# Batched 64x64 products: GpSimd issues a tile's load between the halves of its memset, and eight result buffers in place of six

## The chip, the core and the metric

The kernel runs on one core of a Trainium2 chip. The metric is device time in microseconds (us). Lengths inside one execution are read from its profile, whose span (first to last instruction) is shorter than the time by about 1.8 us. In the profile's lines DVE is VectorE, ACT ScalarE, POOL GpSimd and SP SyncE; the DMA queue q0 is GpSimd's, q1 SP's and q10 ACT's. A line of a timeline has start, us, engine, source line, operation, tiles, sizes and count, and in brackets the idle time before it and what ended it.

## The reference

```python
def setup_inputs():
    return {
        "a": np.random.randn(1024, 64, 64).astype(np.float32),
        "b": np.random.randn(1024, 64, 64).astype(np.float32),
    }

def reference(a, b):
    return np.matmul(a, b).astype(np.float32)
```

Each input and the result is 16.78 MB. Some 50.3 MB have to cross HBM.

## The kernel before

The 1024 products go through in sixteen tiles t of 64. Two tiles share one a tile s of 128 matrices, a(0) to a(7). GpSimd loads a(1) to a(7), four pieces each, and converts to bf16 on the way; a(0) is loaded as fp32 by the SP and ACT queues, which also load the b tiles. VectorE regroups an a tile, PE transposes it, ScalarE copies the transposed tile out, and VectorE spreads it into a block-diagonal tile, the stationary operand of the products. ScalarE evacuates the first half of each result tile and VectorE the second. GpSimd issues the stores, held back by one tile.

```python
    A_AHEAD = 3      # buffers of a tiles
    B_AHEAD = 4      # buffers of b tiles
    HOLD = 2         # the store of tile t is issued after tile t+1 is multiplied
    ...
    o_pool = ctx.enter_context(tc.tile_pool(name="o_pool", bufs=6))
    ...
    def load_a(s):
        a_sb = a_pool.tile([128, 4, 16, 64], bf16, name="a_sb")
        for h in range(4):
            nc.gpsimd.dma_start(
                out=a_sb[:, h, :, :].rearrange("p v k -> p (v k)"), in_=a_v[s, h]
            )
    ...
        load_first_a()                                # a(0), SP and ACT queues
        ...
        for t in range(B_AHEAD):
            load_b(t)
        nc.vector.memset(bd_tiles[0][:], 0.0)
        make_identity(nc, identity)                   # GpSimd
        nc.gpsimd.memset(bd_tiles[1][:], 0.0)         # GpSimd, 4096 elements a row
        for s in range(1, A_AHEAD):
            load_a(s)                                 # a(1), a(2)
        ...
        for t in range(n_t):
            ...
            if half == 0:
                if s + 2 < n_s:
                    regroup(s + 2)                    # VectorE, ahead of multiply(t)
                if s + 1 + A_AHEAD < n_s:
                    load_a(s + 1 + A_AHEAD)
            multiply(t)
            ...
            if t >= HOLD - 1:
                store(t - HOLD + 1)
```

## Time and profile before

| | |
|---|---|
| time, median of 4 runs of the first comparison | 135.51 us (135.26 to 135.67) |
| span of the traced execution | 134.0 us |
| VectorE busy | 105.5 us, 79% |
| HBM traffic | 33.55 MB read, 16.78 MB written, 375 GB/s over the span |
| memset on GpSimd | 3.51 us, first a issue at 4.71 us |
| first packet of GpSimd's DMA queue | 8.6 us |

### The profile page before, as it was taken

To read this page: it belongs to the slowest core of one execution; us is meant where nothing else is said; L and a number is where in the kernel's file an instruction comes from. 1 tells how busy PE (TensorE), PEld (TensorE's weight loads), DVE (VectorE), ACT (ScalarE), POOL (GpSimd) and SP (SyncE) were. 2 spreads that over 40 slices of the span, in tenths; PEclk is the share of its full clock that TensorE was granted. 3 is DMA by queue.
4 is the path that set the end of the run, shared out by engine and by line. 5 is a ranking of instruction groups with operands and counts; after the bars stand their busy time and mean duration, and the time that the engine had idled before them with its cause. 6 is when DMAs were issued, how large, how long until landed. Compare 5 with 4: busy or idle time off the path is not lost.

```text
span 134.0 us, 2820 instructions
## 1 busy us (share of the span) xinstructions
PE 66.2 (49%) x1152; PEld 61.9 (46%) x1152; DVE 105.5 (79%) x145; ACT 86.4 (64%) x125; POOL 43.7 (33%) x55
## 2 busy tenths in 40 slices
PE   0008206903970495849734863696309564466300
PEld 0008106904960485749624752685209463456300
DVE  5720539169899989998999999999299999999940
ACT  3244343991899287959998796679708999363500
POOL 8981215332313240214322244324004031141460
PEclk9999975797799768686998699559955999555555
DMA  3999999999999999999999999999999999999793
GB/s 67 386 360 305 306 284 273 267 301 305 302 280 289 281 396 332 310 289 350 402 359 279 269 367 399 351 270 275 390 397 395 393 397 398 402 406 362 262 313 112
DMA packets 17484, 43.17 MB, mean 322 GB/s; under 512 B 1088, under 2 KB 1088, under 8 KB 17472
## 3 DMA queue, kind: packets, MB, share of 16 engines
q0 software_dynamic: 8448, 24.12, 61.7%
q1 hardware_dynamic: 6624, 13.63, 28.7%
q10 hardware_dynamic: 2400, 5.24, 10.3%
q8 instruction: 9, 0.15, 0.4%
q14 instruction: 3, 0.02, 0.0%
HBM read 33.55 MB, written 16.78 MB: 375 GB/s over the span
## 4 chain that ended last, share of the span: by engine, by line
DMA 62%; DVE 14%; issue 11%; POOL 9%; POOLq 1%; DVEq 0%
DMA a_sb<-in_a_dram 45%; DMA out_dram<-o_sb 17%; DVE o_sb L165 8%; DVE at_bd L121 6%; POOL out_dram L154 3%; POOL a_sb L67 3%; POOL at_bd L205 3%; POOLq L262 1%; POOL identity masks.py:199 0%; DVE a_bf L99 0%; POOL identity masks.py:197 0%; POOLq L154 0%; DVEq L99 0%; POOLq masks.py:199 0%; DVEq L121 0%
## 5 line engine op out<-in xcount | busy, mean ns | idle before, releaser
L177 PEld LDWEIGHTS <-at_bd 128*128 128x128 bf16 x1024 | 43.8, 114 | 45.3 <-DVE o_sb L165 30.4
L177 PE MATMUL o_ps<-b_bf,at_bd 128*128 128x64 bf16 x960 | 43.1, 215 | 40.2 <-DVE o_sb L165 28.5
L121 DVE COPY at_bd<-at_sb 32x1024 f32<-32x1024 f32 x64 | 46.6, 728 | 7.3 <-ACT at_sb L111 5.3
L165 ACT COPY o_sb<-o_ps 64x512 f32<-64x512 f32 x60 | 34.8, 580 | 17.4 <-PE o_ps L177 10.7
L165 DVE COPY o_sb<-o_ps 64x512 f32<-64x512 f32 x60 | 41.3, 689 | 2.2 <-PE o_ps L177 1.3
L154 POOL DMA_DIRECT2D out_dram<-o_sb x20 | 20.9, 1044 | 46.6 <-DVE o_sb L165 22.8
L108 PE MATMUL at_ps<-identity,a_bf 128*128 128x128 f32 x128 | 22.8, 339 | 17.6 <-ACT a_bf L97 10.6
L67 POOL DMA_DIRECT2D a_sb<-in_a_dram x28 | 18.7, 681 | 38.9 <-DMA a_sb<-in_a_dram 28.1
L132 ACT CAST b_bf<-b_sb 128x2048 bf16<-128x2048 f32 x15 | 28.6, 1908 | 3.5 <-DMA b_sb<-in_b_dram 3.5
L108 PEld LDWEIGHTS at_ps<-identity,a_bf 128*128 128x128 f32 x128 | 19.1, 181 | 17.9 <-issue 10.6
L111 ACT COPY at_sb<-at_ps 128x512 f32<-128x512 f32 x32 | 17.8, 588 | 8.3 <-PE at_ps L108 8.1
L99 DVE COPY a_bf<-a_sb 128x4096 bf16<-128x4096 bf16 x7 | 8.6, 1227 | 9.0 <-DMA a_sb<-in_a_dram 8.8
L97 ACT CAST a_bf<-o_sb 128x1024 bf16<-128x1024 f32 x2 | 2.1, 1044 | 4.6 <-DMA o_sb<-in_a_dram 4.6
L165 ACT COPY o_sb<-at_ps 64x256 f32<-64x256 f32 x8 | 2.9, 367 | 3.1 <-PE at_ps L177 3.0
L177 PE MATMUL at_ps<-b_bf,at_bd 128*128 128x64 bf16 x64 | 3.6, 242 | 1.3 <-DVE at_bd L121 1.3
L203 DVE MEMSET at_bd<- 128x4096 f32 x1 | 3.5, 3472 | 0.8 <-issue 0.8
L97 DVE CAST a_bf<-o_sb 128x1024 bf16<-128x1024 f32 x2 | 1.5, 764 | 3.0 <-DMA o_sb<-in_a_dram 3.0
L205 POOL MEMSET at_bd<- 128x4096 f32 x1 | 3.5, 3509 | 0.0
L165 DVE COPY o_sb<-at_ps 64x256 f32<-64x256 f32 x8 | 3.4, 422 | 0.1
L200 ACT ACT_TABLE_LOAD x1 | 1.3, 1283 | 2.3 <-issue 2.3
L139 ACT CAST b_bf<-b_sb 128x512 bf16<-128x512 f32 x2 | 1.1, 614 | 0.4 <-DMA b_sb<-in_b_dram 0.4
L137 DVE CAST b_bf<-b_sb 128x512 bf16<-128x512 f32 x2 | 0.8, 426 | 0.0
(9 smaller groups left out, 1.5 us busy)
## 6 DMA issues: line engine op xcount, KB each, us to landing
out_dram<-o_sb POOLq DMA_DIRECT2D x14, 1024.0 KB, 22.5
a_sb<-in_a_dram POOLq DMA_DIRECT2D x28, 256.0 KB, 19.9
o_sb<-in_a_dram ACTq DMA_DIRECT2D x2, 512.0 KB, 6.9
o_sb<-in_a_dram SPq DMA_DIRECT2D x2, 512.0 KB, 5.9
out_dram<-o_sb POOLq DMA_DIRECT2D x2, 512.0 KB, 6.2
out_dram<-o_sb POOLq DMA_DIRECT2D x4, 256.0 KB, 3.9
b_sb<-in_b_dram SPq DMA_DIRECT2D x12, 0.5 KB, 20.2
b_sb<-in_b_dram ACTq DMA_DIRECT2D x4, 0.5 KB, 16.2
```

Source lines behind the costliest of these rows:

```text
L67: nc.gpsimd.dma_start(out=a_sb[:, h, :, :].rearrange("p v k -> p (v k)"), in_=a_v[s, h])
L97: copy(a_bf[:, :, h, :], a_sb[h].rearrange("p (v k) -> p v k", v=16))
L99: nc.vector.tensor_copy(a_bf[:], a_sb[:].rearrange("p h v k -> p v h k"))
L108: nc.tensor.transpose(at_ps[:, vo, :], a_cols[:, 4 * vo + 2 * j + wl, :], identity[:])
L111: nc.scalar.copy(at_tiles[s][:, j, :, wl, :, :], at_ps[:].rearrange("p vo (g mp) -> p g mp vo", mp=4),)
L121: nc.vector.tensor_copy(bd[rows, :, :, :, h, :].rearrange("p j g wl mo -> p j (g wl) mo"), at_tiles[t // 2][rows, :, half, :, :, :].rearrange(
L132: nc.scalar.copy(b_bf[:], b_sb[:])
L154: nc.gpsimd.dma_start(out=o_v[t, :, lo : lo + n, :], in_=o_sb[:, lo : lo + n].rearrange("p gh j wl n -> p (gh j wl n)"),)
L165: copy(dst, src)
L177: nc.tensor.matmul(o_ps[:, gl, g % 2, j, :], at_bd[:, j, g, :, u], b_bf[:, g, 64 * u : 64 * u + 64], start=(u == 0), stop=(u == 1),)
L203: nc.vector.memset(bd_tiles[0][:], 0.0)
L205: nc.gpsimd.memset(bd_tiles[1][:], 0.0)
```

## The change

GpSimd's 3.5 us memset stood in front of all its a loads. The change cuts it in two and issues a(1) between the halves; a(2) still follows the second half. Two more result buffers are to let evacuation run further ahead of the stores.

```diff
-    o_pool = ctx.enter_context(tc.tile_pool(name="o_pool", bufs=6))
+    o_pool = ctx.enter_context(tc.tile_pool(name="o_pool", bufs=8))
...
-        nc.gpsimd.memset(bd_tiles[1][:], 0.0)
-        for s in range(1, A_AHEAD):
+        nc.gpsimd.memset(bd_tiles[1][:, 0], 0.0)
+        load_a(1)
+        nc.gpsimd.memset(bd_tiles[1][:, 1], 0.0)
+        for s in range(2, A_AHEAD):
             load_a(s)
```

## The prediction

> **What bounds the kernel now.** I read the page's slices first, then the chain of waits, then VectorE's timeline where the chain names it, then the queues stretch by stretch.
>
> ```profile
> DVE  5720539169899989998999999999299999999940
> DMA  3999999999999999999999999999999999999793
> ```
>
> The DMA row is full from the second slice (a slice is 134.0/40 = 3.35 us) to the third from the end. VectorE is ragged for eight slices (27 us), then full to the end with one hole, the 2 in slice 29. So there are two limits that nearly agree: the transfers over the whole span, and VectorE from about 28 us on. The chain says what starts VectorE and what makes the hole:
>
> ```profile
> 1.31 3.46 POOL at_bd L205
> 4.76 3.83 POOL a_sb L67 x7
> 8.59 19.32 DMA a_sb<-in_a_dram
> ...
> 76.67 19.88 DMA a_sb<-in_a_dram
> ```
>
> The columns are start, us, what. The chain begins with GpSimd's 3.46 us memset, goes through its eight DMA issues, and then waits 19.32 us for the last piece of the second tile that they load, a(2). VectorE's own lines show the same two landings, 27.92 and 96.55, as its only long waits after the start:
>
> ```profile
> 28.04 1.23 DVE L99 COPY a_bf<-a_sb 128x4096 bf16<-128x4096 bf16 x1 [4.18 <-DMA a_sb<-in_a_dram]
> 96.58 1.23 DVE L99 COPY a_bf<-a_sb 128x4096 bf16<-128x4096 bf16 x1 [2.56 <-DMA a_sb<-in_a_dram]
> 125.31 3.49 DVE L165 COPY o_sb<-at_ps 64x256 f32<-64x256 f32 x8
> ```
>
> The first is the regrouping of a(2), the second that of a(7), the last a tile. Between 28.04 and 128.80 (125.31 + 3.49) VectorE's other gaps of 0.1 us or more are 0.46, 0.40 and 0.48 us. After 128.80 there are only the last stores. So the time is: landing of a(2), then VectorE's work with one 2.56 us hole for a(7), then 4 to 5 us of stores.
>
> Is a transfer starved anywhere? Busy time by stretches, columns PE, PEld, DVE, ACT, POOL, clock, DMA share, GB/s:
>
> ```profile
> 5.00:8.60 3.60, 0.00 (x0) 0.00 (x0) 0.88 (x2) 1.04 (x1) 3.60 (x8) 1.00 1.02 414
> 8.60:18.00 9.40, 3.65 (x16) 3.28 (x16) 3.47 (x5) 3.39 (x5) 2.50 (x5) 1.00 1.08 305
> 126.00:127.00 1.00, 0.00 (x0) 0.00 (x0) 0.97 (x3) 0.00 (x0) 1.00 (x2) 0.50 0.14 45
> ```
>
> From 5 us the engines are full, so an a tile that starts sooner fills no hole; it takes turns from the b loads. The one hole is at 126 to 127: the stores queued so far have drained and VectorE's last tiles are not out yet. The queues in two stretches, packets, MB, share (8.6 to 18 us, then 18 to 27.7 us):
>
> ```profile
> q0 software_dynamic: 491, 0.91, 50.9%
> q1 hardware_dynamic: 487, 0.97, 30.0%
> q10 hardware_dynamic: 491, 0.99, 27.5%
> ```
>
> ```profile
> q0 software_dynamic: 683, 1.24, 67.3%
> q1 hardware_dynamic: 688, 1.37, 41.1%
> ```
>
> GpSimd's queue q0 takes one packet in three while three queues have work and one in two when two do. It moves 0.91/9.4 = 97 KB per us in the first case and 1.24/9.7 = 128 KB per us in the second, counted as the bf16 that is written. From 5.0 to 8.6 us it moves nothing: its first issue began at 4.71 us, its first packet is at 8.6.
>
> **What the Trainium skill says.** "DMA: Bandwidth & Descriptors", section "Queues, rings and completion order": each DMA engine round-robins between the queue rows with work, packet by packet. The trace agrees: 491, 487 and 491 packets. The same page, "Issuing engines are not separate DMA queues": more issuers save only issue time, since all share the same 16 engines. That too agrees: the DMA share stays at 1.0 to 1.1 whoever issues. "Perfetto Trace Analysis", section "DMA Instruction — SWDGE (GPSIMD)": the end of such an issue is the end of descriptor writing, not of the transfer. The trace agrees, 0.53 to 1.19 us an issue against 7.4 to 24.5 us to landing; so I time this change by landings. "SBUF — State Buffer", section "Who interferes with whom": copies and casts of VectorE in a two-port mode lock GpSimd out, a VectorE instruction outside those modes does not; the page does not list a memset among those that do. I expect no clash from the 3.47 us VectorE memset that will now overlap the issues; no row of this trace shows it.
>
> **The change, part by part.**
>
> (1) The memset of 4096 elements in 3.51 us becomes two of 2048, 1.75 us each by halving. The first a(1) issue moves from 4.71 to 1.25 + 1.76 = 3.0 us, 1.7 us earlier. The four issues of a(1) took 687, 612, 548 and 568 ns of mostly overlapping time, 2.3 us from 4.71 to 7.03. So the second half of the memset runs at about 5.3 to 7.1 us and a(2) is issued from about 7.1, against 7.03 before: not earlier. The block-diagonal tile that the memset clears is first written by VectorE at 21.02 us, so its later end costs nothing.
>
> (2) If the lag from issue to first packet stays 8.6 - 4.71 = 3.9 us, q0 starts at 6.9. The two other queues then have all of a(0) not yet landed, so they give way first: a(0)'s last quarter lands later than 9.5 us, by my estimate 1.5 to 2 us (1.7 us in which its queue drops from 0.82/3.6 = 228 to about 105 KB per us leaves 210 KB, or 2 us at 105). The transposes of a(0) move from 10.6 to about 12.5, VectorE's spread of it from 14.94 to about 16.8, and b(0) from a landing at 18.41 to about 20. None of this reaches VectorE's start: spread of a(0), regrouping of a(1) and spread again are 2.83 + 1.23 + 2.84 = 6.9 us, ending at 23.7 where a(2) is awaited until 27.9. It only eats the 4.18 us gap.
>
> (3) What a(2) gains. q0 gets 1.7 us x 97 = 165 KB more early. The ACT queue's b(1) ends 2 us later, and in those 2 us q0 has a third instead of a half: 2 x (128 - 97) = 62 KB back. Net about 100 KB, which at 128 KB per us is 0.8 us: a(2) lands at about 27.1.
>
> (4) What the end gains. q0 is a queue in order that always has work (each of its issues up to 76.67 us waits for a landing or a store's data while some 20 us of transfers stand queued), so it keeps its 100 KB lead. At its mean rate over 28 to 96.6 us, 11.08 MB/68.6 us = 162 KB per us, a(7) lands 0.6 us earlier. VectorE reaches that point 0.8 us earlier and waits 2.8 instead of 2.6 us. Its end moves from 128.80 to about 128.1. The stores can follow: the hole at 126 to 127 us, 0.9 us, is just what an earlier VectorE closes. Sum: 0.6 to 0.8 us.
>
> (5) Eight result buffers. A result tile waits for the store of the tile six before. This shows twice in ScalarE's lines, 1.75 us before the evacuation at 84.50 and 4.32 us before that at 100.56. VectorE is without a gap over both: 84.98 and 100.64 start where the instructions before them end. So I give the buffers 0 by themselves, at most 0.2 us as a help to (4). With two more, those tiles wait for stores landed 16 us sooner, and both waits go.
>
> **The rivals.** *Bytes alone decide.* The HBM traffic is 33.55 + 16.78 MB, and from 2.2 to 126 us the DMA engines have no hole. If total bytes set the end, advancing a only delays b, and the time stays 135.5. For it: the full DMA row; b(15) lands at 114.12, 0.1 us before its cast. Against it: the hole at 126 us, and VectorE's unbroken work after 96.58. *The start loses what a(1) gains.* If a(0) and b(0) come later by more than 2 to 3 us, because q0 starts even sooner (a lag of 1.3 us, as the late stores have, would put the first packet at 4.3), then PE reaches the first product later than now (22.98 us) and VectorE's first evacuation, not a(2), ends its wait. Slack is about 29.28 - 25.98 = 3.3 us, so the cost is at most 0.5 us, time about 136. *A larger gain.* If q0 starts by 5.5 us, it leads by 200 KB and a(7) comes 1.2 us earlier; with the hole at 126 us closed the stores then run without a gap and no more than about 1.4 us can be had: 134.1. *The wait is elsewhere.* If the first packet at 8.6 us hangs on the eighth issue (it begins at 8.59), nothing moves: 135.5.
>
> **Range and chances.** (4) gives 0.7 us; the larger gain and the two neutral rivals stand about equally to both sides, so I say 134.7 us. Low is 133.6 (the larger gain plus 0.5 for the buffers), high 135.6 (nothing). 2% is 2.7 us, twice what the hole at the end lets through; a loss of 2% needs a delay at the start that outruns 3 us of slack. Chances: faster 0.03, within 2% 0.95, slower 0.02.
>
> **What would show it.** In the profile after: two GpSimd memsets near 1.75 us and a first a issue near 3.0 (1); first q0 packets near 6.9, a(0)'s last cast about 2 us later (2); VectorE's regrouping of a(2) near 27.1 instead of 28.04 (3); that of a(7) near 95.9, a VectorE end near 128.1, and a filled hole before the last stores (4); no ScalarE wait for a store, VectorE none the shorter (5). I am wrong if the two memset halves or the issues between them stretch beside VectorE's memset, if q0's start does not follow its issue, or if a(7) comes no earlier though a(2) does.

## More of the kernel before

The lines that carry the bound stand in the prediction. Two more matter later. The first is of the waits of SP, the engine that issues most b loads; the second is of ScalarE's waits. The columns are who waited for whom, total us, times, longest us.

```profile
SPq L88 <- ACT b_bf L132: 31.2, 7, 6.4
...
ACT o_sb L165 <- DMA out_dram<-o_sb: 6.1, 2, 4.3
```

The first says that a b load often waits for ScalarE's cast of an earlier b tile to free a buffer: the b stream is paced by the computation. The second is the wait that more result buffers take away.

## The result and the profile after

The time is 135.29 us, median of 4 runs (134.93 to 135.43), against 135.51 us. The ratio is 0.9981, interval 0.9956 to 1.0006. A ratio is the mean time of one kernel's fast runs over that of the other's fast runs of the same rounds, so it is not quite the ratio of the medians. Forecast were 0.8 us less; measured are 0.2 to 0.3, in these four runs not clear of the scatter.

The chain of waits of the changed kernel (start, us, what):

```profile
1.30 1.75 POOL at_bd L205
3.05 2.27 POOL a_sb L67 x4
5.32 2.25 POOL at_bd L207
7.57 1.51 POOL a_sb L67 x3
9.08 18.32 DMA a_sb<-in_a_dram
...
75.99 19.89 DMA a_sb<-in_a_dram
```

The start went as planned: half a memset, four issues, the other half. The a(1) issues begin at 3.00 us instead of 4.71. The second half takes 2.31 us (2.25 of them on the chain) against 1.80 for the first, and a(2)'s issues begin at 7.52 us, later than the 7.03 of before. VectorE's regrouping of a(2) and of a(7), and its last instructions:

```profile
27.52 1.23 DVE L99 COPY a_bf<-a_sb 128x4096 bf16<-128x4096 bf16 x1 [4.15 <-DMA a_sb<-in_a_dram]
95.90 1.23 DVE L99 COPY a_bf<-a_sb 128x4096 bf16<-128x4096 bf16 x1 [1.91 <-DMA a_sb<-in_a_dram]
124.63 3.49 DVE L165 COPY o_sb<-at_ps 64x256 f32<-64x256 f32 x8
```

In this pair of traces a(2) is 0.52 us earlier and a(7) and VectorE's end 0.68 us, and the span is 0.6 us shorter: almost the forecast. But the pair flatters the change. The traced execution before took 135.82 us, 0.3 above its kernel's median; the traced one after took 135.21, a little under its own. Stretches of the trace after:

```profile
5.00:8.60 3.60, 0.00 (x0) 0.00 (x0) 0.83 (x2) 1.04 (x1) 3.60 (x5) 1.00 1.04 387
125.20:126.20 1.00, 0.00 (x0) 0.00 (x0) 0.97 (x3) 0.11 (x1) 1.00 (x2) 1.00 0.41 152
```

The DMA engines were full at 5 to 8.6 us before and are full now. The hole ahead of the last stores did not close: it moved, from 126 to 127 us before (DMA share 0.14) to 125.2 to 126.2 now (0.41).

### The profile page after: what moved, and what is told of

Its sections match the earlier page's. It is cut to its first block, busy times and chain, and to the rows that moved or that the text cites. A ratio compares the mean times of both kernels' runs of the same rounds, so it can differ in the third digit from the quotient of the medians.

```text
span 133.4 us, 2815 instructions
## 1 busy us (share of the span) xinstructions
PE 69.4 (52%) x1152; PEld 65.2 (49%) x1152; DVE 105.2 (79%) x145; ACT 86.5 (65%) x125; POOL 43.4 (33%) x56
## 4 chain that ended last, share of the span: by engine, by line
DMA 61%; DVE 13%; issue 12%; POOL 10%; POOLq 1%; DVEq 0%
DMA a_sb<-in_a_dram 45%; DMA out_dram<-o_sb 16%; DVE o_sb L165 7%; DVE at_bd L121 6%; POOL out_dram L154 3%; POOL a_sb L67 3%; POOL at_bd L207 2%; POOL at_bd L205 1%; POOLq L264 1%; POOL identity masks.py:199 0%; DVE a_bf L99 0%; POOL identity masks.py:197 0%; POOLq L154 0%; DVEq L99 0%; POOLq masks.py:199 0%
## 5 line engine op out<-in xcount | busy, mean ns | idle before, releaser
L177 PEld LDWEIGHTS <-at_bd 128*128 128x128 bf16 x1024 | 46.1, 117 | 41.8 <-DVE o_sb L165 28.1
L177 PE MATMUL o_ps<-b_bf,at_bd 128*128 128x64 bf16 x960 | 45.2, 220 | 36.9 <-DVE o_sb L165 26.2
L121 DVE COPY at_bd<-at_sb 32x1024 f32<-32x1024 f32 x64 | 46.1, 720 | 7.6 <-ACT at_sb L111 5.7
L154 POOL DMA_DIRECT2D out_dram<-o_sb x20 | 20.3, 1016 | 48.4 <-DVE o_sb L165 19.9
L108 PE MATMUL at_ps<-identity,a_bf 128*128 128x128 f32 x128 | 24.0, 352 | 17.1 <-ACT a_bf L97 11.0
L108 PEld LDWEIGHTS at_ps<-identity,a_bf 128*128 128x128 f32 x128 | 20.2, 187 | 17.4 <-issue 17.4
L207 POOL MEMSET at_bd<- 128x2048 f32 x1 | 2.3, 2308 | 0.0
L205 POOL MEMSET at_bd<- 128x2048 f32 x1 | 1.8, 1799 | 0.0
```

The lines of the kernel that those rows point to most:

```text
L108: nc.tensor.transpose(at_ps[:, vo, :], a_cols[:, 4 * vo + 2 * j + wl, :], identity[:])
L121: nc.vector.tensor_copy(bd[rows, :, :, :, h, :].rearrange("p j g wl mo -> p j (g wl) mo"), at_tiles[t // 2][rows, :, half, :, :, :].rearrange(
L154: nc.gpsimd.dma_start(out=o_v[t, :, lo : lo + n, :], in_=o_sb[:, lo : lo + n].rearrange("p gh j wl n -> p (gh j wl n)"),)
L177: nc.tensor.matmul(o_ps[:, gl, g % 2, j, :], at_bd[:, j, g, :, u], b_bf[:, g, 64 * u : 64 * u + 64], start=(u == 0), stop=(u == 1),)
L207: nc.gpsimd.memset(bd_tiles[1][:, 1], 0.0)
```

## The experiments

All ratios are to the kernel before, from five rounds on one chip unless said otherwise. Kernels with a wrong result are marked; all others were correct.

**The change again, and each part alone.** The first is the changed kernel unaltered. The parts are the split with six buffers, and the buffers with the whole memset.

```diff
 # split only: the changed kernel, but
+    o_pool = ctx.enter_context(tc.tile_pool(name="o_pool", bufs=6))
 # buffers only: the kernel before, but
+    o_pool = ctx.enter_context(tc.tile_pool(name="o_pool", bufs=8))
```

> The changed kernel once more, for a tighter ratio and a second trace. Theory LEAD (the span is the landing of a(7) plus 37.5 us, as in both traces: 96.55 + 37.49 and 95.87 + 37.5; an earlier first a piece moves that landing): ratio 0.995 to 0.997, a(7) landing 0.4 to 0.7 us before that of the kernel before. Rival BYTES (the total of bytes sets the end and the 0.6 us between the two traces is the spread of runs): ratio 0.999 to 1.001 and a landing of a(7) anywhere between 95.7 and 96.7.

> Only the memset split, six buffers. LEAD: same as the whole change, ratio 0.995 to 0.998, since VectorE never waited for a result buffer; the two ScalarE waits for a store (1.75 and 4.32 us before) are still there. BUFFERS rival (the gain comes from the result buffers): ratio 1.000.

> Only eight result buffers. LEAD: ratio 0.999 to 1.001, a(7) at 96.5 as before, both ScalarE waits for stores gone. BUFFERS rival: ratio 0.996 to 0.998.

| | ratio | 95% interval | first q0 packet | regrouping of a(2) | of a(7) |
|---|---|---|---|---|---|
| change again | 0.9978 | 0.9954 to 1.0001 | 7.15 us | 27.71 | 96.10 |
| split only | 0.9980 | 0.9957 to 1.0002 | 7.12 us | 27.55 | 95.56 |
| buffers only | 1.0005 | 0.9981 to 1.0028 | 8.63 us | 27.97 | 96.54 |

The changed kernel's 0.9978 lies between the two ranges expected for it. The buffers do nothing: their ratio is 1.0005, though ScalarE's two waits for stores are gone from the trace. With the split alone they are still there, at no cost:

```profile
ACT o_sb L165 <- DMA out_dram<-o_sb: 4.5, 2, 3.8
```

Whatever there is comes from the split. Over all 16 runs with it the mean is 135.14 us, over all 48 runs of the kernel before in the rounds 135.37: 0.23 us less. The 48 include three chips on which neither kernel with the split ran; the 15 of the same comparisons have 135.43, so the gain is 0.2 to 0.3 us.

**A larger head start.** All eight issues of a(1) and a(2) ahead of the whole memset, eight buffers.

```diff
-        nc.gpsimd.memset(bd_tiles[1][:], 0.0)
         for s in range(1, A_AHEAD):
             load_a(s)
+        nc.gpsimd.memset(bd_tiles[1][:], 0.0)
```

> Eight buffers, and GpSimd issues all eight pieces of a(1) and a(2) before its whole memset: first issue near 1.3 us instead of 3.0. LEAD: with the lag of 4 us seen twice the first packet is near 5.3, q0 leads the kernel before by about 3.4 us x 97 KB less what it gives back, some 200 KB, a(7) lands 1.1 to 1.3 us earlier, ratio 0.990 to 0.993, unless a(0) comes so late that VectorE's first evacuation and not a(2) ends its wait (then 0.995 to 1.0). BYTES: 0.999 to 1.001.

The ratio is 0.9978 (0.9956 to 1.0001), no better than the split. GpSimd's first packet came at 5.47 us, twice the head start, yet VectorE's regrouping of a(2) and of a(7) began no earlier than with the split:

```profile
27.56 1.23 DVE L99 COPY a_bf<-a_sb 128x4096 bf16<-128x4096 bf16 x1 [4.40 <-DMA a_sb<-in_a_dram]
...
95.72 1.23 DVE L99 COPY a_bf<-a_sb 128x4096 bf16<-128x4096 bf16 x1 [1.90 <-DMA a_sb<-in_a_dram]
```

The price showed at once: a(0)'s last cast began at 10.87 us instead of 9.49 and the first cast of b at 20.65 instead of 18.43. But VectorE still waited for a(2), so the price is not why the head start brought nothing; the tables under "Where the lead goes" show what became of it.

**A later start.** The memset done twice, eight buffers.

```diff
         nc.gpsimd.memset(bd_tiles[1][:], 0.0)
+        nc.gpsimd.memset(bd_tiles[1][:], 0.0)
```

> Kernel before with eight buffers and the whole memset done twice: first a issue near 8.2 us, 3.5 us later. If the lead of GpSimd's queue counts as measured for the split (1.42 us of earlier first packet gave 0.35 us), 3.5 us later cost 0.9 us: ratio 1.006 to 1.009, regrouping of a(2) 1.0 to 1.8 us later than 28.0. If BYTES alone decide: 0.999 to 1.001.

The ratio is 1.0086 (1.0069 to 1.0102), as expected by the lead theory, but the trace tells another story. VectorE's lines:

```profile
31.19 1.23 DVE L99 COPY a_bf<-a_sb 128x4096 bf16<-128x4096 bf16 x1 [4.17 <-DMA a_sb<-in_a_dram]
...
97.08 1.23 DVE L99 COPY a_bf<-a_sb 128x4096 bf16<-128x4096 bf16 x1
```

The regrouping of a(2) is 3.15 us later than before, yet a(7)'s last share landed at 96.52 us, where it landed before (96.55). The second line has no wait: VectorE itself was late. The kernel became 1 us slower because VectorE, which started 3.15 us later, had more work left than the wait for a(7) could absorb, not because a(7) was late.

**Where the lead goes.** The KB that GpSimd's queue q0 had moved by a given time, summed from the packets of the traces (at 95 us its stores are in it):

| KB by | 10 us | 18 us | 22 us | 27.5 us | 95 us |
|---|---|---|---|---|---|
| before | 129 | 893 | 1403 | 2114 | 12809 |
| changed | 241 | 996 | 1476 | 2175 | 12868 |
| loads first | 325 | 1079 | 1552 | 2237 | 13140 |
| memset twice | 0 | 494 | 1005 | 1716 | 12748 |

The lead of the changed kernel is 112 KB at 10 us, 103 at 18 and 61 at 27.5, and it is still 59 at 95. The tail experiments below with ScalarE's tail, one of them with large last stores, have the changed kernel's program up to tile 14, so they count as well: over five traces with the split the lead over the four without it is 68 KB at 27.5 us and 48 at 95, where the four differ among themselves by 106. At q0's 162 KB per us, 48 KB are 0.3 us (an estimate).

The memset done twice has a deficit of 398 KB at 27.5 us and of 61 at 95: most of it is made up, unasked. A lead does not shrink in the same way: that of the loads issued first grows to 331 KB at 95 us. Why it brought nothing shows in the 16 shares of a piece, one for each DMA engine; a piece has landed when the last share has. The shares of the last piece, us:

| | median share | second slowest | last |
|---|---|---|---|
| a(2), four traces without the split | 27.62 to 27.74 | 27.77 to 27.87 | 27.85 to 28.11 |
| a(2), five with it | 27.01 to 27.14 | 27.14 to 27.39 | 27.19 to 27.76 |
| a(2), loads first | 26.60 | 26.78 | 27.44 |
| a(7), four without the split | 94.05 to 94.51 | 95.17 to 95.68 | 95.50 to 96.55 |
| a(7), five with it | 93.82 to 94.12 | 95.35 to 95.58 | 95.51 to 96.08 |
| a(7), loads first | 92.84 | 94.36 | 95.69 |

With the loads first, 15 of 16 shares keep the head start to the end, about 1 us at a(7). One share does not (whether it is always that of the same engine, the trace does not tell): it is 0.66 us behind the next slowest at a(2) and 1.33 at a(7), and VectorE waits for it. The shares of a(1)'s first piece already lay 1.07 us apart, against 0.46 in the kernel before. Why one share starts late is open.

**The worth of an early turn.** a(0) loaded in 2 KB rows instead of 4 KB rows, the rest as in the changed kernel.

```diff
-        parts = [raw[h % 2][:, 1024 * (h // 2) : 1024 * (h // 2) + 1024] for h in range(4)]
+        parts = [
+            raw[h % 2].rearrange("p (c i n) -> p i c n", c=2, i=2)[:, h // 2] for h in range(4)
+        ]
...
-            (nc.scalar if h % 2 else nc.sync).dma_start(out=parts[h], in_=a_v[0, h])
+            (nc.scalar if h % 2 else nc.sync).dma_start(
+                out=parts[h], in_=a_v[0, h].rearrange("g m (c n) -> g m c n", c=2)
+            )
```

> The changed kernel with a(0) loaded in 2 KB rows instead of 4 KB rows (same bytes, same issues). Theory TURNS (queues take turns by packet, so against 4 KB packets of a(0) GpSimd's 2 KB turn is worth about 67 KB per us and not the 97 of the prediction): its queue has by 10 us about 270 KB instead of 240, a(0)'s last cast is 0.3 to 0.8 us later, regrouping of a(2) 0.1 to 0.3 us earlier; ratio 0.995 to 0.998. If packet size does not matter: 240 KB at 10 us as in the changed kernel.

The queues at 7.1 to 8.6 us (packets, MB, share), first in the changed kernel, then in this one:

```profile
q10 hardware_dynamic: 63, 0.26, 42.5%
q0 software_dynamic: 51, 0.10, 36.5%
q1 hardware_dynamic: 60, 0.15, 28.1%
```

```profile
q0 software_dynamic: 64, 0.13, 45.9%
q10 hardware_dynamic: 95, 0.19, 33.8%
q1 hardware_dynamic: 89, 0.16, 30.6%
```

In the changed kernel q10's 63 packets hold 0.26 MB, 4.1 KB each, and q0's 51 hold 0.10 MB, 2.0 KB each: a turn by packet is worth half as much against a(0). From its first packet to 8.6 us q0 moved 99 KB in 1.41 us, 70 KB per us; with short rows 121 KB in 1.26 us, 96 KB per us. That is the 97 that the prediction had used. So the turns are shown. They bring no time: ratio 0.9990 (0.9969 to 1.0010), a(0)'s last cast at 11.66 us (1.8 us after that of the changed kernel, where 0.3 to 0.8 were expected), regrouping of a(2) at 27.70, no earlier. Of the 270 KB expected at 10 us, 260 were measured.

**What a(7) waits for: the b loads.** The changed kernel with two b tiles loaded by half, 1.05 MB fewer, the half used twice (wrong result).

```diff
-        queue.dma_start(out=b_sb[:], in_=b_v[t])
+        rows = 8 if t in (6, 8) else 16
+        queue.dma_start(out=b_sb[:, :rows], in_=b_v[t][:, :rows])
...
+            if t in (6, 8):
+                nc.scalar.copy(b_bf[:, 0:8, :], b_sb[:, 0:8, :])
+                nc.scalar.copy(b_bf[:, 8:16, :], b_sb[:, 0:8, :])
```

> The changed kernel with the same 1.05 MB fewer b bytes (wrong result on purpose). BYTES theory for a(7)'s landing (what a(7) waits for is the b bytes that share the DMA engines, not how early GpSimd's queue started): a(7) lands 1.5 to 2.5 us earlier than the 95.5 to 96.1 of the split kernels, VectorE's hole before it shrinks to under 0.5 us, ratio 0.983 to 0.990. If a(7) follows the head start alone: landing 95.5 to 96.1, ratio 0.996 to 0.999.

The ratio is 0.9858 (0.9830 to 0.9887), 1.9 us. VectorE's regrouping of a(7):

```profile
92.41 1.23 DVE L100 COPY a_bf<-a_sb 128x4096 bf16<-128x4096 bf16 x1
```

There is no wait before it; a(7) had landed at 91.03 us, over 4 us earlier, and VectorE ended at 125.28. This is more than the 2.6 us that 1.05 MB take at 400 KB per us: q0's own mean rate over most of the kernel is 162 KB per us, so if all the freed turns fell to q0 it would be 6.5 us, and the truth lies between (all three are estimates). What b takes from the same engines over 95 us weighs more on a(7) than any head start tried here. The run also splits two casts in two and may free two b buffers sooner, so the bytes alone are not separated. And b is not all: holding the stores back (below) lands a(7) 3.5 us earlier with every byte of b.

**How much chance is in a(7).** The kernel before, traced twice more (no rounds, one look).

> The kernel before, traced again. If chance makes up half of the 0.7 us: an execution near 135.4 us with the regrouping of a(7) at 96.1 to 96.3. If the split is worth 0.7 us in every execution: 96.4 to 96.7 whatever its time.

> The same once more: regrouping of a(2) at 27.9 to 28.1 in both, and the span the regrouping of a(7) plus 37.2 to 37.6 us.

These executions took 134.95 and 135.13 us. From the first and then from the second trace:

```profile
28.05 1.23 DVE L99 COPY a_bf<-a_sb 128x4096 bf16<-128x4096 bf16 x1 [3.91 <-DMA a_sb<-in_a_dram]
95.77 1.23 DVE L99 COPY a_bf<-a_sb 128x4096 bf16<-128x4096 bf16 x1 [1.92 <-DMA a_sb<-in_a_dram]
```

```profile
28.23 1.23 DVE L99 COPY a_bf<-a_sb 128x4096 bf16<-128x4096 bf16 x1 [4.15 <-DMA a_sb<-in_a_dram]
...
95.53 1.23 DVE L99 COPY a_bf<-a_sb 128x4096 bf16<-128x4096 bf16 x1 [1.20 <-DMA a_sb<-in_a_dram]
```

Both regrouped a(7) earlier than either expectation for the first had it, and the second missed the expected a(2) and span by 0.1 us. Without the split, four traces have a(2) regrouped at 27.97 to 28.23 (mean 28.07), with it three have 27.52 to 27.71 (mean 27.59): 0.48 us, clear of the scatter. For a(7) the four are 95.53 to 96.58 (mean 96.10) and the three 95.56 to 96.10 (mean 95.85): 0.25 us, inside a scatter of 1.05 us between executions without the split. With the two traces of ScalarE's tail (27.31 and 27.88, 95.53 and 95.73) the differences are 0.48 and 0.34 us. That agrees with the 0.2 to 0.3 us of the times.

**The slowest share.** The shares of a(7)'s last piece landed between 93.73 and 96.55 us in the first trace of the kernel before, the median at 94.05; up to 35 us such a spread is under 0.6 us in this trace. It jumps to 2.1 us at the piece that lands at 37.79, right after PE's first 16 KB instruction fetch (35.8 us, 0.98 us on one DMA engine). I suspected the fetches. The changed kernel with only the first of each pair of products (wrong result):

```diff
-                    for u in range(2):
+                    for u in range(1):
...
-                            start=(u == 0),
-                            stop=(u == 1),
+                            start=True,
+                            stop=True,
```

> The changed kernel with only the first of each pair of products (wrong result on purpose): 1024 PE rows fewer, so of the nine 16 KB instruction fetches about four are gone. Theory STRAGGLER (a tile lands when the last of its 16 shares lands; from 36 us on one or two DMA engines are 2 to 3 us behind because each fetch takes one of them for 1 us): the spread between the first and the last share of a(7)'s last piece falls from 2.2 to 2.8 us to under 1.6, its last share lands 0.7 to 1.5 us earlier than in the changed kernel (under 95.2), ratio to the kernel before 0.986 to 0.993. Rival LEAD or BYTES (all engines alike): spread and landing as in the changed kernel, ratio 0.996 to 0.999.

The ratio is 0.9966 (0.9952 to 0.9981), 0.0012 below the change again. The fetch queue, before and in this kernel:

```profile
q8 instruction: 9, 0.15, 0.4%
```

```profile
q8 instruction: 5, 0.08, 0.2%
```

Four of nine fetches are gone, but the spread of a(7)'s last piece is 2.69 us and its last share lands at 95.82, as in the changed kernel (2.38, 95.87). Only the second slowest share gained (94.79 instead of 95.57). The theory in this form fell: the four later fetches don't set a(7)'s landing. The first, which stays, is still suspect. In two traces it came some 7 us sooner (29.21 us in the second trace of the kernel before, 28.13 with ScalarE's tail), and in both the first piece with a late share landed sooner too, at 31.74 and 30.95. But with the loads first a share was late before any fetch, and no run takes the first fetch away, so its part is not shown.

**The tail.** Stores held back one tile more, so that a(7) is issued ahead of one more store, in the changed kernel:

```diff
-    HOLD = 2
+    HOLD = 3
```

> The changed kernel with stores held back one tile more, so that a(7)'s pieces are issued ahead of one more 1 MB store. A(7) theory (the span is a(7)'s landing plus 37.5 us until VectorE's 1.9 us hole is gone): a(7) lands 3 us or more earlier, the hole is gone, VectorE ends near 126.3, and the time falls by 1.0 to 1.9 us: ratio 0.985 to 0.991. Rival: the stores then drain later and their tail takes the place of the hole: ratio 0.995 to 1.0 with no DMA hole before the last stores.

Regrouping of a(7) and two stretches of this kernel:

```profile
93.40 1.23 DVE L99 COPY a_bf<-a_sb 128x4096 bf16<-128x4096 bf16 x1
```

```profile
114.00:121.00 7.00, 4.43 (x80) 4.27 (x81) 6.77 (x11) 4.89 (x10) 2.13 (x2) 0.50 1.02 404
122.00:130.00 8.00, 0.06 (x2) 0.00 (x0) 3.54 (x9) 0.73 (x2) 3.59 (x5) 0.50 1.00 350
```

VectorE's hole is gone, it ends at 125.68, 2.4 us before the changed kernel, and the DMA engines have no hole. And the ratio is 1.0016 (1.0000 to 1.0033). The last store lands at 131.91 us against 131.93 in the changed kernel: with VectorE out of the way the bytes still to be stored set the end. The span is 0.2 us under that of the kernel before (133.38 against 133.56, means); the time outside the span is 2.19 instead of 1.81 us, which no trace explains. The ratio is worse than either expectation; that no DMA hole is left is what the rival had said.

The other way to end VectorE sooner, from the tail itself: ScalarE evacuates the second half of tile 14.

```diff
-                copy = nc.vector.tensor_copy if half else nc.scalar.copy
+                on_vector = half and t != n_t - 2
+                copy = nc.vector.tensor_copy if on_vector else nc.scalar.copy
```

> The changed kernel with the second half of the last tile but one evacuated by ScalarE, which idles there, instead of VectorE (right result): VectorE's last instruction ends about 2.2 us sooner, near 126. VECTOR theory (the tail follows VectorE's end): ratio 0.985 to 0.991. BYTES or SLOW-ENGINE theory: the hole before the last stores closes, but the last share of the last store lands at 131.2 to 131.9, ratio 0.993 to 0.998.

VectorE ended at 126.08, 2 us sooner, the hole closed, the last store landed at 131.50, and the ratio is 0.9996 (0.9967 to 1.0024). The landing is in the range that the theories of bytes and of a slow engine had given; the gain of 0.2 to 0.7% that they had expected is missing, but for the traced run (134.77 us, the shortest of six).

Two runs took something away from the floor that the held-back stores met: the four fetches, and the 1.05 MB of b (both wrong results).

> Stores held back one tile more and only the first of each pair of products (wrong result on purpose): four of the nine 16 KB instruction fetches gone, VectorE done by about 125.7. SLOW-ENGINE theory (the floor met by holding stores back is the one or two DMA engines that also carry the fetches and are never idle): the last store lands 0.7 us or more before the 131.9 of the kernel with stores held back, ratio to the kernel before 0.991 to 0.996. ALL-BYTES theory (all 16 engines are full; the fetches are 0.06 of 50 MB): last landing within 0.4 us of 131.9, ratio 0.998 to 1.002.

> Stores held back one tile more and 1.05 MB fewer b bytes: two of the sixteen b tiles are loaded by half and that half is used twice (wrong result on purpose; ScalarE's cast of them becomes two). BYTES theory (with VectorE done at 125.7, the bytes set the end): 1.05 MB at about 400 KB per us is 2.6 us; the time falls by 1.5 to 2.6 us, until VectorE's end plus its last stores bounds it: ratio 0.982 to 0.990. If bytes are not the limit: as with stores held back alone, 1.000 to 1.003.

Fewer fetches gave 0.9993 (0.9969 to 1.0018): by the ratio the slow-engine theory missed and all-bytes held. The trace says the opposite, with the last store at 131.20 us, 0.7 before that of the held-back stores; but it is of the shortest of six runs (134.80 us, median 135.34). So this one is not settled. Fewer b bytes gave 0.9927 (0.9905 to 0.9949), 1.2 us below the held-back stores, short of the expected 0.982 to 0.990. The DMA engines then have a hole again (share 0.42 from 121.4 to 123.4 us), so bytes no longer bound this tail.

The last four asked why the tail is slow: 350 KB per us after 122 us against 404 before it. The suspects were the small stores, since tile 14 goes out in halves and tile 15 in quarters.

```diff
 # large last (held-back stores, or ScalarE's tail): tile 14 whole, tile 15 in halves
-            held[t] = [lambda q=q: put(2 * q, 2) for q in range(4)]
+            held[t] = [lambda q=q: put(4 * q, 4) for q in range(2)]
-            whole = t < n_t - 2
+            whole = True
 # both tail changes: whole = True alone;  all halves: whole = False
```

> Stores held back one tile more, tile 14 stored whole and tile 15 in two halves instead of two halves and four quarters. SMALL-STORES theory (the floor is the lower rate of half and quarter stores): the last 2 MB move at 390 KB per us or more, the last store lands 0.8 us or more before 131.9, ratio 0.990 to 0.996. END theory (the rate falls towards the end whatever the size of the stores): 330 to 365 KB per us still, ratio 1.000 to 1.006.

> ScalarE evacuates the second half of tile 14, and tile 14 is stored whole, tile 15 in two halves. SMALL-STORES: last 2 MB at 390 KB per us or more, ratio 0.990 to 0.996. END: ratio 0.999 to 1.006.

> Stores held back one tile more, ScalarE evacuates the second half of tile 14, tile 14 stored whole, tile 15 in quarters. SMALL-STORES: half the effect of the two runs above, ratio 0.994 to 0.998. END: 0.999 to 1.003.

> The changed kernel with every tile but the last stored as two halves. SMALL-STORES: stores in the stretch 114 to 120 us move at 330 to 365 KB per us instead of 405, the kernel is 1 to 4 us slower, ratio 1.008 to 1.03. END: 405 KB per us in that stretch as before, ratio 0.996 to 1.004.

| | ratio | 95% interval |
|---|---|---|
| held-back stores, large last | 1.0012 | 0.9987 to 1.0038 |
| ScalarE's tail, large last | 0.9973 | 0.9952 to 0.9995 |
| both, tile 14 whole | 0.9989 | 0.9966 to 1.0012 |
| all halves | 1.0054 | 1.0024 to 1.0083 |

The stretches of the kernel with all halves:

```profile
114.00:120.00 6.00, 3.04 (x64) 2.73 (x64) 5.80 (x9) 3.11 (x6) 2.35 (x3) 0.66 1.03 404
122.00:130.00 8.00, 2.49 (x47) 2.33 (x44) 5.79 (x12) 2.90 (x8) 3.59 (x5) 0.50 0.93 330
```

The ratios of three of the four fell between the ranges of the two theories, so the rates have to decide. Halves move 404 KB per us in the middle, so the size of the stores is not the cause, and the theory of small stores fell. Nor did large last stores speed the tail: 346 KB per us from 122 to 130 us with held-back stores. The rate falls near the end whatever is done to the stores; why stays open. So does why all halves cost 1.0054, about 1 us more than the changed kernel. No version here beats the changed kernel clearly: ScalarE's tail with large last stores has 0.9973, the changed kernel 0.9978 when run again.

## Why the prediction was wrong

It named the right parts and forecast within 2%, which held; the size was wrong, 0.8 us against 0.2 to 0.3. By its steps:

- **(1)** held for the issue (3.00 us). The second memset half, forecast at 1.75 us, took 2.31, and a(2)'s issues came 0.5 us later than before. That cost nothing: a(2) stands behind a(1) in the same queue.
- **(2)** held in direction. The lag from issue to first packet was 4.2 us, not 3.9, so q0 started 1.42 us earlier instead of 1.7. a(0)'s last cast moved by 0.4 us, not 2, and b(0) by 0.8.
- **(3) is the first step that failed, by its size:** "1.7 us x 97 = 165 KB" measured 112 KB at 10 us, because the turn is by packet and a(0)'s packets are twice as large (70 KB per us; short rows restored 96). The give-back of 62 KB measured 51. "Net about 100 KB" measured 61, and a(2) came 0.48 us earlier over all traces instead of 0.8.
- **(4) failed with it:** "so it keeps its 100 KB lead". There were 61 to 68 KB to keep, and 48 are left at 95 us in the mean of the traces, inside their scatter of 106. a(7) came 0.25 to 0.34 us earlier instead of 0.6. And a lead in bytes is not yet an earlier landing: with the loads first 331 KB of lead brought a(7)'s last share no further than the split did. How a deficit is made up, as it was with the memset done twice, is not shown; that b loads wait for casts suggests that their queues then leave turns to q0.
- From a(7) on the chain held: VectorE ended 32.22 us after it began to regroup a(7), in both traces of the pair. So what a(7) gains is what the kernel gains.
- **(4), second half:** "the hole at 126 to 127 us, 0.9 us, is just what an earlier VectorE closes" was wrong as well. The hole moved with the stores ahead of it, and only became shallower. And ending VectorE 2 us earlier by other means gained nothing, since the last bytes then set the end.
- **(5)** held: the buffers are worth nothing.
- **The rivals.** "Bytes alone decide" was the nearest: it said 135.5, and the time was 135.3. It was set aside because VectorE's chain after a(7) is unbroken. That chain is real, but its start is a landing, and in full DMA engines an early turn moved that landing by 0.3 us only. The prediction also named a stretched memset half as a sign of being wrong; it came (2.31 us), beside a cast and not beside VectorE's memset, and did no harm.

## What to carry to other kernels

When the DMA engines are full, a transfer issued earlier only changes whose turn it is, and a turn is worth the bytes of a packet; ask what sets the landing that the critical engine waits for late in the kernel, not only the first one. A lead in bytes helps only if the slowest share has it too. Before a small gain is read off a pair of traces, see how far the same landing differs between executions of one program: here 1.05 us, three to four times the effect. And moving one bound (VectorE, by 2.4 us) is worth what the next bound leaves, here nothing.

## What the Trainium skill lacked or had wrong

- "DMA: Bandwidth & Descriptors", section "Queues, rings and completion order", has the round-robin by packet but not what follows when packets differ in size: against 4 KB packets a queue with 2 KB packets moved 70 KB per us, against 2 KB packets 96.
- The same page, section "Latency and other measured facts", gives about 1 us to the first byte of a GpSimd DMA. Here it was 3.9 to 4.2 us from the start of the issue in the kernels before and after, where the DMA engines were nearly or quite full, but also 4.0 with the loads issued first, where their share was 0.15 to 0.76 in the first 1.5 us, and 5.2 with the memset done twice. Why is open.
- "SBUF — State Buffer", section "Who interferes with whom": VectorE's memset beside four DMA issues did no harm (685, 562, 556 and 576 ns beside it; 687, 612, 548 and 568 in the kernel before, where it ended during the first), as the page lets expect. The lock that the page describes for casts fits the second memset half: where VectorE's cast came first (5.08 to 5.19 us, ten traces) the cast took 0.69 to 0.76 us and the memset 2.31 to 2.35; where it came later (5.19 to 5.43, four traces) the memset took 1.87 and the cast 2.26 to 2.49. What the page does not give is the cost here: about 0.5 us for the one or 1.7 for the other.
- "Runtime: NRT & Kernel Launch", section "Instruction fetch mechanics", calls the cost of a 16 KB instruction block mostly hidden. Here each of PE's nine fetches held one DMA engine for about 1 us, and soon after the first one share of an a piece landed about 1 to 2 us after the others. That the fetch is the cause is not shown; taking four later ones away did not shorten the spread.
- No page has the fall of the store rate near the end, from 404 to 346–358 KB per us while the DMA engines stayed full (share 0.97 to 1.01), nor the 0.3 us by which some kernels' time outside the span differs (1.8 or 2.1 to 2.2 us). Both causes are open.
